# A gated DeltaNet kernel on one core: where the row coefficients of the triangular inverses are applied, and which engines make the right-hand sides

## The chip, the core and the metric

The kernel runs on one core of a Trainium2 chip. The core has a matrix engine (TensorE, in the profile PE, with its weight loads listed as PEld), a vector engine (VectorE, DVE), a scalar or activation engine (ScalarE, ACT), a general engine (GpSimd, POOL) and a queue engine that issues transfers (SyncE, SP). Each engine takes its instructions in order from its own queue and waits on semaphores for the others. The metric is the device time of one execution in microseconds (us), the median of several.

## What is computed

The reference is a two-layer diffusion backbone over 512 latent tokens and 256 context tokens of 1024 channels. Layer 0 mixes tokens with four bidirectional gated DeltaNet heads beside four pooling groups, layer 1 with convolutions; behind each mixer stands a ConvFFN. The change lies in the DeltaNet heads, and there in one term:

```python
def _gdn_chunk_terms(k, v, g, beta):          # per chunk of 64 tokens
    kb = k * beta
    a_mat = jnp.where(strict, jnp.einsum('bhnck,bhnsk->bhncs', kb, k) * decay, 0.0)
    rhs = jnp.concatenate([v * beta, kb * jnp.exp(gc)[..., None]], axis=-1)
    sol = lax.linalg.triangular_solve(a_mat + jnp.eye(GDN_CHUNK), rhs, left_side=True,
                                      lower=True, unit_diagonal=True)
```

Every chunk, head and direction needs the inverse of a unit triangular 64 x 64 matrix, whose off-diagonal part is the product of the keys with themselves, times a decay, times a coefficient beta for each row. The state recurrence then runs over the chunks, forward and backward.

## The kernel before, in words

**Matmuls.** The dense products are made in three passes. `piece` (L162) splits a block of weights: ScalarE writes the high part (L167), then GpSimd or VectorE the low part (L173). `gemm` (L210) issues the three products (L219).

**Order of the work.** Layer 0's mixer is a list of steps, `PLAN`: `b0 k0 k1 e0 q0 n0 e1 q1 v0 g0 i0 n1 v1 g1 x0 p0 p1 r1 ...`. The heads go in two pairs. `k` makes the keys, `e` (`systems`) their products with themselves times the decay, `m` (tile name `kk`), and the row coefficients `bl`, one table for each of three levels; `q` the queries. `e` ends with a small inverse of the 16 x 16 diagonal blocks (`base_inverse`), a serial chain on VectorE behind two transfers, whose result `gc` comes back from memory. `i0` runs the six inverse chains of head pair 0, three at a time; `x0` runs the two directions of pair 0's recurrence together with the six inverse chains of pair 1, four generators at a time; `r1` is pair 1's recurrence. In the trace these steps lie from about 150 to 330 us. Most instructions are put in order for each engine by the framework's scheduler, from the order of the code and the dependences; a few are pinned. Among the pinned ones are the products of `ada_rest` (L362) on VectorE, which reduce rows of a large weight for the modulation vectors: 24 are run inside `x0`, 16 inside `r1`, others in the output projection that follows (about 340 to 360 us).

**One inverse chain** (`inverse`, L974) doubles the inverted blocks three times, from 16 to 128 rows. Each level needs two matrix products. The first (`it_ps`, L991) multiplies `m` with a right-hand side `r1`, the second (`iv_ps`, L999) multiplies the masked result `it` (VectorE L993, at the last level ScalarE L995) with a right-hand side `r2`. The inverse `g` is then updated by VectorE (L1004) or, at the last level, ScalarE (L1002), and TensorE transposes it (L1006) to make the next level's `r1`. `r1` carries the row coefficients: it is the transposed inverse, times `bl` of the level, times a mask of zeros and ones. Since `bl` is a different scalar for each of the two heads, VectorE makes `r1` in two instructions of 128x128, one for each head: the first from `gc` (L984), those of the two later levels from PSUM (L1009). `r2` carries no coefficient, and GpSimd makes it in one instruction of 128x256 (L986 at first, L1011 later).

**Beside it.** `queries` squares the queries on ScalarE (`q_sq`, L1022), sums them on TensorE (`qn_ps`, L1025) and ends on VectorE (`qss`, L1036). The recurrence's ScalarE copies with a scale for each head, `kd` (L1069) and `vn` (L1089), each 128x128, run beside the chains of pair 1. Tiles of 128x256 come from rings: tag `inv` has ten buffers, three for each chain, tag `z` three.

Of the kernel before, what the change touches and what calls it, by code (L numbers as in the profile page):

```python
# [10 lines left out]
AF = mybir.ActivationFunctionType  # L11
# [3 lines left out]
P = 128  # L15
# [17 lines left out]
MUL, ADD, SUB = ALU.mult, ALU.add, ALU.subtract  # L33
# [81 lines left out]
class Kernel:  # L115
# [852 lines left out]
    def inverses(self, p, s):  # L968
        s["g"] = [self.t2("mg", "g") for _ in range(3)]
        two = lambda x, c: x[c // 2][:, 2 * (c % 2):2 * (c % 2) + 2]  # L970
        return [self.inverse(two(s["m"], c), s["gc"][:, :, 2 * c:2 * c + 2], s["bl"][:, :, 2 * c:2 * c + 2],
                             two(s["g"], c)) for c in (0, 1, 2, 5, 3, 4)]

    def inverse(self, m, gc, bl, g):  # L974


        nc = self.nc
        v4 = lambda x: x.rearrange("p q (b c) -> p q b c", c=16)
        mk = lambda m: m.rearrange("p (b c) -> p b c", c=16)
        mk4 = lambda m: mk(m)[:, None, :, :].broadcast_to([P, 2, 8, 16])  # L980
        gk = lambda k: gc[:, k][:, :, None, :].broadcast_to([P, 2, 8, 16])
        r1, r2, t = (self.t1("inv", nm) for nm in ("r1", "r2", "it"))
        for h in range(2):
            nc.vector.scalar_tensor_tensor(out=mk(r1[:, h]), in0=gc[:, 1, h][:, None, :].broadcast_to([P, 8, 16]),  # L984
                                           scalar=bl[:, 0, h:h + 1], in1=mk(self.par[:, 0]), op0=MUL, op1=MUL)
        nc.gpsimd.tensor_tensor(out=v4(r2), in0=gk(0), in1=mk4(self.par[:, 0]), op=MUL)  # L986
        nc.gpsimd.tensor_tensor(out=v4(g), in0=gk(0), in1=mk4(self.blk), op=MUL)
        for lv in range(3):
            pt = self.gd4("it_ps")
            for h in range(2):  # L990
                nc.tensor.matmul(out=pt[:, h], lhsT=m[:, h], rhs=r1[:, h], start=True, stop=True)  # L991
            if lv < 2:
                nc.vector.tensor_tensor(out=t, in0=pt[:, 0:2], in1=self.mask(self.lvl[:, lv], 2), op=MUL)  # L993
            else:
                nc.scalar.copy(out=t, in_=pt[:, 0:2])  # L995
            yield 1
            ps = self.gd4("iv_ps")
            for h in range(2):
                nc.tensor.matmul(out=ps[:, h], lhsT=t[:, h], rhs=r2[:, h], start=True, stop=True)  # L999
            if lv == 2:  # L1000
                for a, c in ((slice(0, 64), slice(64, P)), (slice(64, P), slice(0, 64))):
                    nc.scalar.activation(out=g[a, :, c], in_=ps[a, 0:2, c], func=AF.Copy, scale=-1.0)  # L1002
                break
            nc.vector.tensor_tensor(out=g, in0=g, in1=ps[:, 0:2], op=SUB)  # L1004
            for h in range(2):
                nc.tensor.transpose(out=ps[:, 2 + h], in_=g[:, h], identity=self.ident)  # L1006
            yield 1
            for h in range(2):
                nc.vector.scalar_tensor_tensor(out=r1[:, h], in0=ps[:, 2 + h], scalar=bl[:, lv + 1, h:h + 1],  # L1009
                                               in1=self.par[:, lv + 1], op0=MUL, op1=MUL)  # L1010
            (nc.gpsimd if R2 else nc.vector).tensor_tensor(out=r2, in0=g, in1=self.mask(self.par[:, lv + 1], 2), op=MUL)  # L1011

    def queries(self, p, s):
# [431 lines left out]
```

## Time and profile before

| | |
|---|---|
| time, median of 3 runs | 1320.72 us (1320.23 to 1323.22) |
| the profiled execution's own time | 1324.16 us |
| its span in the trace | 1322.4 us |
| mean granted TensorE clock | 0.981 |
| busy: TensorE, VectorE, GpSimd, ScalarE | 1262.9, 913.2, 669.1, 582.5 us |

A profile is one execution. Its page lists each engine's busy time, the span in 40 slices with the busy share in tenths (PEclk is the clock that TensorE was granted), the chain of work that ended last, and groups of instructions. A group's row reads: line, engine, operation, output tile and input tiles, shape, count, then busy time and the mean duration in ns, then the engine's idle time just before these instructions and what released it. A view of windows gives, for stretches of the span, each engine's busy time and count, the granted clock and the transfers' share.

### The profile page before, as it was taken

The page shows a single profiled execution, that of the slowest core. Times are in us where ns is not written, and L with a number is a line of the kernel's source. Part 1 is how long each engine was busy: PE and PEld are TensorE (multiplying, and loading weights), DVE is VectorE, ACT ScalarE, POOL GpSimd, SP SyncE. Part 2 cuts the span into 40 slices and gives each one's busy share as a digit, 9 for nine tenths or more (in the row PEclk, how much of TensorE's full clock was granted, in tenths as well). Part 3 has the DMA queues.
Part 4 walks back from the last instruction along what each step waited for, and adds up shares of the span by engine and source line. Part 5 has one row for each costly group of instructions (what it writes and reads, how often), then busy time and mean ns, then how long its engine had stood idle before and what let it go on. Part 6 is the DMA issues. An engine that isn't in the chain of part 4 may idle for free.

```text
span 1322.4 us, 19555 instructions
## 1 busy us (share of the span) xinstructions
PE 1262.9 (95%) x6690; PEld 1065.1 (81%) x6690; DVE 913.2 (69%) x1874; ACT 582.5 (44%) x1091; POOL 669.1 (51%) x607
## 2 busy tenths in 40 slices
PE   6998889989899999999999999899999999999996
PEld 2877878877798888888888988688988888888886
DVE  3778899998777878788444669847786666661135
ACT  3545324455547333333322685435653333332235
POOL 2355466666426555555354567954243434433452
PEclk8998899999999999999999999999999999999998
DMA  9511213431633656666565523234032233333334
GB/s 358 196 50 40 66 44 105 144 119 33 201 103 94 195 194 195 196 193 204 171 196 161 163 88 95 66 96 128 18 112 97 95 99 100 96 92 96 96 115 130
DMA packets 100340, 166.58 MB, mean 126 GB/s; under 512 B 20432, under 2 KB 25616, under 8 KB 100240
## 3 DMA queue, kind: packets, MB, share of 16 engines
q1 hardware_dynamic: 89280, 164.09, 38.5%
q10 hardware_dynamic: 10960, 1.25, 0.7%
q8 instruction: 53, 0.87, 0.3%
q14 instruction: 47, 0.39, 0.1%
HBM read 162.60 MB, written 2.69 MB: 125 GB/s over the span
## 4 chain that ended last, share of the span: by engine, by line
PE 65%; DVE 5%; ACT 2%; POOL 2%; issue 1%; DMA 1%; POOLq 0%; ACTq 0%; SPq 0%; DVEq 0%
PE prod_ps L219 40%; PE out_ps L219 20%; PE half_ps L219 3%; PE ln_e L417 1%; DVE z L478 1%; POOL w_lo L173 1%; PE ln_w L427 1%; DVE ln_d L424 1%; DMA ada_w<-in_ada 0%; DVE ada_w L362 0%; DVE ln_s L404 0%; DVE al L457 0%; ACT ln_u L490 0%; ACT w_hi L167 0%; DVE w_lo L173 0%
## 5 line engine op out<-in xcount | busy, mean ns | idle before, releaser
L173 POOL TENSOR_TENSOR w_lo<-w_raw,w_hi 128x512 fp32r<-128x512 f32 (+1 forms) x302 | 392.9, 1305 | 460.5 <-ACT w_hi L167 441.2
L167 ACT CAST w_hi<-w_raw 128x512 fp32r<-128x512 f32 (+1 forms) x408 | 246.3, 609 | 462.0 <-PE prod_ps L219 145.3
L219 PE MATMUL prod_ps<-uh,w_lo 128*128 128x512 f32 x792 | 309.9, 392 | 4.9 <-POOL w_lo L173 4.9
L219 PE MATMUL prod_ps<-uh,w_hi 128*128 128x512 f32 x792 | 309.7, 391 | 0.0
L219 PE MATMUL prod_ps<-ul,w_hi 128*128 128x512 f32 x792 | 309.4, 391 | 0.0
L604 DVE SCALAR_TENSOR_TENSOR f_acc<-prod_ps,prm,f_acc 128x441 f32<-128x441 f32 (+2 forms) x320 | 222.3, 695 | 61.5 <-ACT f_acc L593 52.2
L219 PEld LDWEIGHTS prod_ps<-uh,w_lo 128*128 128x128 f32 x792 | 149.4, 189 | 36.9 <-POOL w_lo L173 6.0
L219 PEld LDWEIGHTS prod_ps<-ul,w_hi 128*128 128x128 f32 x792 | 149.6, 189 | 31.2
L219 PEld LDWEIGHTS prod_ps<-uh,w_hi 128*128 128x128 f32 x792 | 149.6, 189 | 30.9
L173 DVE TENSOR_TENSOR w_lo<-w_raw,w_hi 128x512 fp32r<-128x512 f32 (+1 forms) x106 | 84.6, 798 | 124.4 <-ACT w_hi L167 120.9
L219 PE MATMUL out_ps<-ah,w_lo 128*128 128x256 f32 (+1 forms) x352 | 118.4, 336 | 4.6 <-DVE w_lo L173 4.6
L219 PE MATMUL out_ps<-ah,w_hi 128*128 128x256 f32 (+1 forms) x352 | 118.6, 337 | 1.6 <-ACT ah L456 1.6
L219 PE MATMUL out_ps<-al,w_hi 128*128 128x256 f32 (+1 forms) x352 | 119.4, 339 | 0.0
L219 PE MATMUL out_ps<-hh,w_lo 128*128 128x512 f32 (+1 forms) x280 | 99.3, 355 | 1.9 <-POOL w_lo L173 1.9
L219 PE MATMUL out_ps<-hh,w_hi 128*128 128x512 f32 (+1 forms) x280 | 98.7, 352 | 0.1
L219 PE MATMUL out_ps<-hl,w_hi 128*128 128x512 f32 (+1 forms) x280 | 98.6, 352 | 0.0
L362 DVE SCALAR_TENSOR_TENSOR ada_w<-ada_w,crow_ps 128x512 f32<-128x512 f32 x112 | 70.7, 682 | 9.8 <-DMA ada_w<-in_ada 9.8
L219 PEld LDWEIGHTS out_ps<-ah,w_lo 128*128 128x128 f32 x352 | 67.2, 191 | 11.9 <-DVE w_lo L173 4.8
L219 PEld LDWEIGHTS out_ps<-ah,w_hi 128*128 128x128 f32 x352 | 67.2, 191 | 8.7 <-ACT ah L456 2.0
L219 PEld LDWEIGHTS out_ps<-al,w_hi 128*128 128x128 f32 x352 | 67.5, 192 | 7.8 <-DVE al L457 0.8
L219 PEld LDWEIGHTS out_ps<-hh,w_lo 128*128 128x128 f32 x280 | 53.4, 191 | 9.9 <-POOL w_lo L173 2.2
L219 PEld LDWEIGHTS out_ps<-hh,w_hi 128*128 128x128 f32 x280 | 53.4, 191 | 7.9 <-ACT w_hi L167 0.3
(362 smaller groups left out, 2290.5 us busy)
## 6 DMA issues: line engine op xcount, KB each, us to landing
w_raw<-in_ffn_up SPq DMA_DIRECT2D x176, 256.0 KB, 2.6
ada_w<-in_ada SPq DMA_DIRECT2D x160, 256.0 KB, 3.7
w_raw<-in_ffn_down SPq DMA_DIRECT2D x100, 256.0 KB, 2.7
w_raw<-in_even_in SPq DMA_DIRECT2D x40, 256.0 KB, 2.7
w_raw<-in_odd_in SPq DMA_DIRECT2D x40, 256.0 KB, 2.8
ada_w<-in_ada SPq DMA_DIRECT2D x16, 512.0 KB, 8.4
w_raw<-in_even_out SPq DMA_DIRECT2D x16, 256.0 KB, 2.7
w_raw<-in_odd_out SPq DMA_DIRECT2D x16, 256.0 KB, 2.6
```

What stands on the lines that cost most here:

```text
L167: r = nc.scalar.copy(out=hi[:, :n], in_=raw)
L173: r = eng.tensor_tensor(out=lo[:, :n], in0=raw, in1=hi[:, :n].bitcast(F32), op=SUB)
L219: r = nc.tensor.matmul(out=o, lhsT=w, rhs=x[k][:, c0:c1], start=clear and k == i == 0, stop=k == n - 1 and i == 2, skip_group_check=pin)
L362: r = nc.vector.scalar_tensor_tensor(out=w, in0=w, scalar=1.0, in1=c, op0=MUL, op1=MUL, accum_out=self.mod[:, k, i:i + 1])
L417: nc.tensor.matmul(out=pe[:, 2 * (n * e + i):2 * (n * e + i) + 2], lhsT=t[:, i * P:(i + 1) * P], rhs=ones, start=e == 0 and i == 0 and not ...
L424: nc.vector.tensor_tensor(out=d[:, 0:n], in0=self.ident[:, None, :].broadcast_to([P, n, P]), in1=x.broadcast_to([P, n, P]), op=MUL)
L427: nc.tensor.matmul(out=o, lhsT=self.ones, rhs=d[:, 0:n].rearrange("p a b -> p (a b)"), start=True, stop=True)
L478: nc.vector.tensor_tensor(out=z, in0=z, in1=x, op=op)
L604: nc.vector.scalar_tensor_tensor(out=o, in0=sv[:, r0 + dr:r1 + dr, q0 + dc:q1 + dc], scalar=w[:, tap:tap + 1], in1=o, op0=MUL, op1=ADD)
```

## The change

The row coefficients move from `r1` to the other factor of the first product. A new function `rows` lets ScalarE write a copy of `m`, scaled with `bl` of the level, one 128x128 activation for each head, into a new tile `mb`; the product takes `mb` in place of `m`. `rows` is called ahead of the first level and, for each next level, before the chain's generator hands over. `r1` is then only a mask times the transposed inverse: the first one is one GpSimd instruction of 128x256, put ahead of the first `r2`; the later ones are one VectorE instruction of 128x256. `mb` is one tile a chain: from tag `z` for head pair 0, from tag `inv` for pair 1.

```diff
         return [self.inverse(two(s["m"], c), s["gc"][:, :, 2 * c:2 * c + 2], s["bl"][:, :, 2 * c:2 * c + 2],
-                             two(s["g"], c)) for c in (0, 1, 2, 5, 3, 4)]
+                             two(s["g"], c), "inv" if p else "z") for c in (0, 1, 2, 5, 3, 4)]
...
-    def inverse(self, m, gc, bl, g):
+    def inverse(self, m, gc, bl, g, tag):
...
-        for h in range(2):
-            nc.vector.scalar_tensor_tensor(out=mk(r1[:, h]), in0=gc[:, 1, h][:, None, :].broadcast_to([P, 8, 16]),
-                                           scalar=bl[:, 0, h:h + 1], in1=mk(self.par[:, 0]), op0=MUL, op1=MUL)
+        mb = self.t1(tag, "mb")
+        def rows(lv):
+            for h in range(2):
+                nc.scalar.activation(out=mb[:, h], in_=m[:, h], func=AF.Copy, scale=bl[:, lv, h:h + 1])
+        rows(0)
+        nc.gpsimd.tensor_tensor(out=v4(r1), in0=gk(1), in1=mk4(self.par[:, 0]), op=MUL)
...
-                nc.tensor.matmul(out=pt[:, h], lhsT=m[:, h], rhs=r1[:, h], start=True, stop=True)
+                nc.tensor.matmul(out=pt[:, h], lhsT=mb[:, h], rhs=r1[:, h], start=True, stop=True)
...
+            rows(lv + 1)
             yield 1
-            for h in range(2):
-                nc.vector.scalar_tensor_tensor(out=r1[:, h], in0=ps[:, 2 + h], scalar=bl[:, lv + 1, h:h + 1],
-                                               in1=self.par[:, lv + 1], op0=MUL, op1=MUL)
+            nc.vector.tensor_tensor(out=r1, in0=ps[:, 2:4], in1=self.mask(self.par[:, lv + 1], 2), op=MUL)
```

Lines behind the change stand five further down in the changed file: `q_sq` at L1022 before is L1027 after. The scheduler moves other instructions along with it. The first place is ScalarE's queue around the squares of the first pair of queries; `ql` are the queries, `vc` values, `w_hi` a split weight.

```order
 L805 ACTIVATE ql<-qkv_ps,prm 128x512
 L167 CAST w_hi<-w_raw 128x512 x2
-L1022 ACTIVATE q_sq<-ql 128x512 x2
+L988 ACTIVATE mb<-kk,bl 128x128 x4
+L1027 ACTIVATE q_sq<-ql 128x512 x2
 L805 ACTIVATE vc<-qkv_ps,prm 128x256
+L988 ACTIVATE mb<-kk,bl 128x128
 L811 ACT_TABLE_LOAD
 L811 ACTIVATE ql<-ql 128x512
```

Four scaled copies now stand ahead of the two squares, and a fifth behind the values.

The second place is GpSimd's queue at the start of `i0`, before the change; L986 is a first `r2`, L987 a first `g`, L1105 a mask of the recurrence.

```order
L932 MEMSET xi 128x512
L986 TENSOR_TENSOR r_1535<-gc,even_k 128x256
L933 MEMSET xi 128x2x16
L987 TENSOR_TENSOR g<-gc,even_k 128x256 x4
L173 TENSOR_TENSOR w_lo<-w_raw,w_hi 128x512 x5
L1105 TENSOR_TENSOR at<-el,even_k 128x256 x2
L986 TENSOR_TENSOR r_1546<-gc,even_k 128x256
L986 TENSOR_TENSOR r_1557<-gc,even_k 128x256
L1011 TENSOR_TENSOR r_1535<-g,even_k 128x256
```

The same place after the change, where L991 is the new first `r1` and L992 the first `r2`:

```order
L932 MEMSET xi 128x512
L991 TENSOR_TENSOR r_1534<-gc,even_k 128x256
L933 MEMSET xi 128x2x16
L992 TENSOR_TENSOR r_1535<-gc,even_k 128x256
L993 TENSOR_TENSOR g<-gc,even_k 128x256 x4
L173 TENSOR_TENSOR w_lo<-w_raw,w_hi 128x512 x4
L991 TENSOR_TENSOR r_1547<-gc,even_k 128x256
L992 TENSOR_TENSOR r_1548<-gc,even_k 128x256
L173 TENSOR_TENSOR w_lo<-w_raw,w_hi 128x512
L1110 TENSOR_TENSOR at<-el,even_k 128x256
L991 TENSOR_TENSOR r_1560<-gc,even_k 128x256
L992 TENSOR_TENSOR r_1561<-gc,even_k 128x256
```

Each chain's first `r1` stands right ahead of its `r2`; the second and third chain's come behind four and five weight splits.

The third place is VectorE's queue near the end of the output projection, before the change; `z` are the residual sums, `ln_s` the sums of the layer norm, and the last row is a split of weights that the next products need.

```order
L524 SCALAR_TENSOR_TENSOR z_3480<-out_ps,mod_g,z_3480 128x512
L362 SCALAR_TENSOR_TENSOR ada_w,mod<-ada_w,crow 128x512
L401 TENSOR_TENSOR ln_s_3621<-ln_s_3621,z_3480 128x512
L404 TENSOR_TENSOR ln_s_3622<-ln_s_3622,ln_sq 128x512
L524 SCALAR_TENSOR_TENSOR z_3481<-out_ps,mod_g,z_3481 128x512
L362 SCALAR_TENSOR_TENSOR ada_w,mod<-ada_w,crow 128x512
L401 TENSOR_TENSOR ln_s_3621<-ln_s_3621,z_3481 128x512
L404 TENSOR_TENSOR ln_s_3622<-ln_s_3622,ln_sq 128x512
L362 SCALAR_TENSOR_TENSOR ada_w,mod<-ada_w,crow 128x512 x2
L173 TENSOR_TENSOR w_lo<-w_raw,w_hi 128x512
```

The same place after the change:

```order
L524 SCALAR_TENSOR_TENSOR z_3528<-out_ps,mod_g,z_3528 128x512
L362 SCALAR_TENSOR_TENSOR ada_w,mod<-ada_w,crow 128x512
L401 TENSOR_TENSOR ln_s_3669<-ln_s_3669,z_3528 128x512
L404 TENSOR_TENSOR ln_s_3670<-ln_s_3670,ln_sq 128x512
L362 SCALAR_TENSOR_TENSOR ada_w,mod<-ada_w,crow 128x512
L524 SCALAR_TENSOR_TENSOR z_3529<-out_ps,mod_g,z_3529 128x512
L371 TENSOR_TENSOR mod_3749<-mod 128x16
L173 TENSOR_TENSOR w_lo<-w_raw,w_hi 128x512
L401 TENSOR_TENSOR ln_s_3669<-ln_s_3669,z_3529 128x512
L404 TENSOR_TENSOR ln_s_3670<-ln_s_3670,ln_sq 128x512
```

The split of the weights, which stood behind three rows of `ada_rest` and the `ln_s` sums of the last `z`, now stands two instructions behind that `z`, ahead of its sums; the rows of `ada_rest` stand further up.

## The prediction

> **What bounds the kernel now.** I read the page first: shares, slices and the chain that ended last.
>
> ```profile
> span 1322.4 us, 19555 instructions
> PE 1262.9 (95%) x6690; PEld 1065.1 (81%) x6690; DVE 913.2 (69%) x1874; ACT 582.5 (44%) x1091; POOL 669.1 (51%) x607
> ...
> PE   6998889989899999999999999899999999999996
> DVE  3778899998777878788444669847786666661135
> ...
> PE 65%; DVE 5%; ACT 2%; POOL 2%; issue 1%; DMA 1%; POOLq 0%; ACTq 0%; SPq 0%; DVEq 0%
> ```
>
> TensorE is busy 95% of the span and carries 65% of the chain that ended last. Over the whole kernel a lighter VectorE is worth nothing; it can pay only where TensorE has gaps. A slice is 33 us, so the inverse chains (150 to 330 us) are slices 5 to 10, where VectorE reads 8, 9, 9, 9, 9, 8. The view of windows gives these stretches, with two earlier and one later one that the new order touches.
>
> ```profile
> core 0: us, PE busy (x) PEld busy (x) DVE busy (x) ACT busy (x) POOL busy (x), PEclk, DMA share, GB/s
> 110.00:114.00 4.00, 1.12 (x10) 1.09 (x10) 3.32 (x6) 3.13 (x6) 2.11 (x2) 1.00 0.12 33
> 114.00:122.00 8.00, 8.00 (x34) 7.24 (x34) 7.41 (x23) 3.49 (x4) 1.76 (x3) 0.57 0.21 66
> 160.00:210.00 50.00, 46.11 (x305) 39.59 (x304) 47.13 (x108) 15.71 (x38) 28.87 (x37) 1.00 0.12 30
> 210.00:280.00 70.00, 65.72 (x457) 57.03 (x456) 65.25 (x182) 27.62 (x81) 48.30 (x57) 1.00 0.39 125
> 350.00:370.00 20.00, 15.36 (x108) 14.76 (x107) 17.29 (x34) 9.23 (x17) 7.84 (x6) 0.91 0.52 167
> ```
>
> Between 160 and 280 us, 120 us in all, VectorE is busy 47.13 + 65.25 = 112.38 and idle 7.62; TensorE is busy 111.83 and idle 8.17. Both are nearly full at once. The 8.17 us are what a faster supply can win here, as the trace counts it. ScalarE is busy 43.33 us of the 120 and GpSimd 77.17. The waits of this stretch tell which gaps are VectorE's; each row is total, times, longest.
>
> ```profile
> ACT w_hi L167 <- PE pool_ps L219: 17.0, 6, 5.8
> ACT it L995 <- PE it_ps L991: 15.0, 11, 7.7
> ...
> PE it_ps L991 <- DVE r L984: 3.6, 7, 1.0
> ...
> PE it_ps L991 <- DVE r L1009: 1.5, 3, 0.8
> ...
> PE k_ps L1064 <- DVE oo L1120: 0.8, 1, 0.8
> ...
> PE o_ps L1109 <- DVE s L1100: 0.7, 1, 0.7
> PE iv_ps L1006 <- DVE g L1004: 0.6, 2, 0.4
> ```
>
> Of the 8.17 us, 3.6 + 1.5 = 5.1 end with exactly the two groups that the change rewrites, and 2.1 with other VectorE work. So the ceiling in this stretch is small, whatever VectorE loses.
>
> **The change part by part.** The groups of the stretch from 160 to 280 us, kept apart by shape, price it.
>
> ```profile
> L362 DVE SCALAR_TENSOR_TENSOR ada_w<-ada_w,crow 128x512 f32<-128x512 f32 x26 | 22.9, 913 | 0.0
> L1011 POOL TENSOR_TENSOR r<-g,even_k 128x256 f32<-128x256 f32 x24 | 20.4, 864 | 11.9 <-DVE g L1004 11.8
> L1009 DVE SCALAR_TENSOR_TENSOR r<-iv_ps,bl,even_k 128x128 f32<-128x128 f32 x48 | 14.0, 340 | 0.5 <-PE iv_ps L1006 0.3
> L993 DVE TENSOR_TENSOR it<-it_ps,even_k 128x256 f32<-128x256 f32 x24 | 10.0, 420 | 2.9 <-PE it_ps L991 2.6
> ```
>
> From 145 to 330 us, which holds all of the first right-hand sides and of the recurrence's scaled copies:
>
> ```profile
> L984 DVE SCALAR_TENSOR_TENSOR r<-gc,bl,even_k 128x128 f32<-128x128 f32 x24 | 13.8, 603 | 4.1 <-DMA gc<-scr 4.1
> ...
> L1089 ACT ACTIVATE vn<-v_ps,nb 128x128 f32<-128x128 f32 x40 | 11.9, 366 | 9.3 <-PE v_ps L1086 9.2
> ...
> L1069 ACT ACTIVATE kd<-k_ps,gc_ex 128x128 f32<-128x128 f32 x40 | 11.0, 385 | 2.3 <-PE k_ps L1064 2.3
> ...
> L986 POOL TENSOR_TENSOR r<-gc,even_k 128x256 f32<-128x256 f32 x12 | 9.4, 792 | 5.2 <-DMA gc<-scr 5.2
> ```
>
> And the lines of the two right-hand sides by themselves, with the shortest, median and longest in ns:
>
> ```profile
> L984 DVE SCALAR_TENSOR_TENSOR r<-gc,bl,even_k x24: 335/490/1392, 149.4 to 261.5; 128x128 f32<-128x128 f32 x24
> L1009 DVE SCALAR_TENSOR_TENSOR r<-iv_ps,bl,even_k x48: 330/340/352, 180.5 to 273.2; 128x128 f32<-128x128 f32 x48
> ```
>
> *The first right-hand side leaves VectorE.* VectorE loses 24 instructions, 13.8 us by the group's busy time. GpSimd gains 12, at the price of its twin L986, 0.79 us each: 9.5 us. In GpSimd's order the new one stands ahead of that twin, and `it_ps` and `iv_ps`, in the rows above, wait for VectorE and never for GpSimd. I therefore let the 3.6 us that TensorE waits for L984 go. What is late next is the first `it_ps` behind GpSimd, where the second and third chain's instruction stands behind four or five splits of weights; a rival prices that. GpSimd's 43 us of idle time in the stretch cover the 9.5 us.
>
> *The later ones become one instruction.* Instead of two of 0.34 us there is one of 128x256 with a PSUM and an SBUF input; L993 has exactly these operands, 0.42 us. VectorE saves 14.0 − 24 × 0.42 = 4.0 us in all. On the chain from `g` to the next `it_ps` the last half is ready 0.26 us sooner, and TensorE waited there three times, 1.5 us: at 0.17 us each (0.26 less something for the first half, which could start early before) I take 0.5.
>
> *What VectorE's 18 us are worth.* VectorE loses 13.8 + 4.0 = 17.8 us, more than twice what TensorE idles here. Beyond the two waits above, the freed time can shorten only the 2.1 us of the other waits on VectorE. I take half, 1.0; the bounds are nothing and 2.1.
>
> *ScalarE's copies.* There are 72 new activations (12 chains, three levels, two heads). The trace has no scaled copy from SBUF to SBUF of this size; the nearest rows are `vn` and `kd`, 128x128 with a scale from PSUM. Each group's busy time over its count, 11.9 / 40 and 11.0 / 40, gives 0.30 and 0.28 us where they follow each other, and the mean is 0.37 alone. So 72 cost 20 to 27 us of ScalarE, which idles 77 us of the 120. I cost them at nothing where they come a level ahead: `mb` needs only `m` and `bl`, known long before. The cover fails where ScalarE's queue stands behind something that waits for TensorE; that is the first rival.
>
> *Four copies ahead of the squares.* This is one place where the copies are on a path. The order has four `mb` ahead of `q_sq`, at 112 us of the trace.
>
> ```profile
> 111.20 1.13 ACT L167 CAST w_hi<-w_raw 128x512 fp32r<-128x512 f32 x2
> ...
> 112.23 1.15 ACT L1022 ACTIVATE q_sq<-ql 128x512 f32<-128x512 f32 x2
> ...
> 112.91 1.05 PE L1025 MATMUL qn_ps<-ones,q_sq 128*128 128x2 f32 x8 [2.88 <-ACT q_sq L1022]
> ...
> 115.95 0.17 DVE L1036 TENSOR_SCALAR qss<-qn_ps 128x8 f32<-128x8 f32 x1
> ```
>
> ScalarE goes straight from the casts to the squares, and TensorE waits 2.88 us for them. Four copies of 0.30 us put the squares 1.2 us later, with nothing to hide it on TensorE, which has nothing else in this window (1.12 us busy of 4). VectorE's `qss` stands in the middle of the serial base inverse, so the delay also moves that chain. I take +1.2; the bounds are 0, if the scheduler's other moves give it back, and 1.5 (4 × 0.37).
>
> The row for 114 to 122 us shows a granted clock of 0.57 right behind that gap. The clock is lowered there already, and I let a longer gap cost itself and no second fall.
>
> *The end of the output projection.* The split of weights that TensorE waits for there moves ahead of two `ln_s` sums and of rows of `ada_rest`.
>
> ```profile
> 351.86 0.68 DVE L401 TENSOR_TENSOR ln_s<-ln_s,z 128x512 f32<-128x512 f32 x1
> 352.46 0.68 DVE L404 TENSOR_TENSOR ln_s<-ln_s,ln_sq 128x512 f32<-128x512 f32 x1
> ...
> 356.41 0.68 DVE L173 TENSOR_TENSOR w_lo<-w_raw,w_hi 128x512 fp32r<-128x512 f32 x1
> ```
>
> and TensorE's side of it:
>
> ```profile
> 357.15 0.46 PE L219 MATMUL out_ps<-ah,w_lo 128*128 128x256 f32 x1 [4.64 <-DVE w_lo L173]
> ```
>
> The rows of `ada_rest` still have to run ahead of it, only earlier; the two sums, 1.36 us, do not. TensorE's 4.64 us can shrink by that, if the rows' transfers don't hold VectorE instead. I take −1.0, between 0 and −1.4.
>
> *Sum.* −3.6 − 0.5 − 1.0 + 1.2 − 1.0 = −4.9 us. Against the profiled execution (1324.16 us, of which 1.8 lie around the span) that is 1319.3. That execution lies 3.4 us above the median of the runs, 1320.72, and I take the sum off the median: 1315.8.
>
> [...] L984, with two operands in SBUF, runs from 335 to 1392 ns, while L1009, with one, keeps within 330 to 352; and L362, two operands from SBUF, has a mean of 913 ns in this stretch. So VectorE's work with two SBUF operands is stretched by something. [...]
>
> **The rivals.**
>
> *Slower: the products wait for ScalarE.* `mb` sits in an in-order queue behind work that itself waits for TensorE: casts that wait for the pooling products (17.0 us in 6 waits, 2.8 each, longest 5.8) and `it` copies of the last level (15.0 us in 11 waits, longest 7.7). Where an `mb` of the next level stands behind one, its chain's `it_ps` comes late by up to that wait, and only three or four chains run beside each other to cover it. Two such exposed waits of 2.9 us undo the 4.9; four give −4.9 + 11.6 = +6.7, about 1327. For it: the copies are made in the same turn as the transposes, just when the level needs them next. Against it: with a level of other chains between, most waits will have passed. 0.18.
>
> *No measurable change: TensorE's order or GpSimd is the bound.* The waits for L984 go, but the first `r1` of the later chains, behind splits of weights on GpSimd, is late in its place, or the gap comes up at the next in-order matmul. The 5.1 us then only change their name, and the sum keeps +1.2 − 1.0: about 1320.5. For it: VectorE and TensorE idle about the same, 7.62 and 8.17. Against it: the first `r1` does not depend on anything that is late. 0.26.
>
> *Faster by more.* Matmuls overlap in the records, so that a busy TensorE may hide slack. Were VectorE the real bound of the stretch, more than half of its 17.8 us would come off: with the other terms about −10, 1310.7. For it: VectorE is 94% busy from 160 to 280 us. Against it: every wait for VectorE there comes to only 7.2 us. 0.14.
>
> **How the numbers follow.** My forecast, −4.9 us with its own range of −3 to −7, has 0.42; the rivals 0.18, 0.26 and 0.14. A measurement of this kernel can tell about 0.2%, 2.6 us. The forecast and the larger gain are faster by more than that: 0.56; no measurable change 0.26; slower 0.18. The range reaches to the larger gain, 1310.0, and on the slow side past no change into the first rival's smaller cases, three exposed waits, −4.9 + 8.7 = +3.8: 1324.0. That leaves out the rest of both tails.
>
> **What would show it.** The waits of TensorE on the first right-hand sides should be gone and no wait of `it_ps` on GpSimd or ScalarE should take their place; a total above 2.9 us there means a rival. `mb` should show 72 activations of 0.28 to 0.37 us, the single product 24 of 0.42 us, the new GpSimd row 12 of about 0.79. VectorE's busy time should fall by about 18 us; if it falls by under 12, the rows of L362 have been stretched. The gap ahead of `qn_ps` should read about 4.1 us instead of 2.88, and the wait of `out_ps` at the end of the projection about 3.6 instead of 4.64. I am wrong if TensorE's waits between 160 and 330 us stay at their sum, or if the place where the time moves lies outside the inverse chains.

## The result, and the profile after

The changed kernel takes 1329.49 us (median of 6, 1324.64 to 1333.74) against 1320.61 (median of 6, 1319.87 to 1323.22): a ratio of 1.0057, 95% interval 1.0038 to 1.0075. It is slower, by 8.9 us of the medians. A second measurement (e1 below) gave 1329.91 against 1321.91, 1.0067 (1.0045 to 1.0088).

The two profiled executions hide this. That of before took 1324.16 us, longer than any of its six runs; that of after took 1324.64, the shortest of its runs. So places are read from the traces, and sizes from the medians. The page of after:

```profile
span 1322.8 us, 19607 instructions
...
PE 1260.1 (95%) x6690; PEld 1063.7 (80%) x6690; DVE 895.3 (68%) x1826; ACT 604.1 (46%) x1163; POOL 680.9 (51%) x619
...
PE   6998899987989999999999999899999999999997
...
DVE  3778897996777887778444669847686666661125
```

VectorE did lose what was forecast, 913.2 − 895.3 = 17.9 us (forecast 17.8), ScalarE gained 21.6 and GpSimd 11.8. TensorE's row is what differs: in its tenth slice, 298 to 331 us, it has a 7 where before had a 9, and the inverse chains are over by then. The windows of after, of the stretch of the chains and of that place:

```profile
core 0: us, PE busy (x) PEld busy (x) DVE busy (x) ACT busy (x) POOL busy (x), PEclk, DMA share, GB/s
160.00:210.00 50.00, 47.31 (x317) 40.97 (x316) 40.57 (x85) 28.03 (x80) 34.70 (x44) 1.00 0.16 43
210.00:280.00 70.00, 63.77 (x457) 56.14 (x455) 65.50 (x171) 37.34 (x115) 53.62 (x60) 1.00 0.41 127
325.00:330.00 5.00, 0.91 (x1) 0.50 (x2) 4.00 (x5) 0.00 (x0) 3.94 (x3) 0.54 0.15 53
330.00:335.00 5.00, 5.00 (x24) 3.53 (x23) 3.37 (x13) 2.17 (x4) 0.00 (x0) 0.78 0.17 52
```

From 160 to 280 us TensorE idles 120 − 111.08 = 8.92 us, where it idled 8.17 before: the lighter VectorE closed no gap of TensorE. Between 325 and 330 us TensorE is busy 0.91 of 5 us, and behind it the granted clock is at 0.54 and 0.78. The waits of after between 145 and 345 us name both:

```profile
ACT mb L988 <- PE it_ps L997: 18.9, 11, 3.7
...
PE pool_y L1192 <- DVE pool_o L1186: 6.7, 1, 6.7
...
DVE pool_o L1181 <- POOL pool_q L1177: 5.7, 1, 5.7
...
PE it_ps L997 <- POOL r L991: 2.0, 1, 2.0
...
PE it_ps L997 <- DVE r L1015: 1.8, 4, 0.6
```

The 5.1 us in which `it_ps` waited for VectorE's right-hand sides have become 2.0 for GpSimd's first one and 1.8 for the new single product. And one wait of 6.7 us is new: `pool_y`, the last product of the fourth pooling, a stage that the diff doesn't touch. How it comes about is in three lines of each trace: the chains' first products, the recurrence's last ones and the poolings' products, with the first and last start. Before:

```profile
L991 PE MATMUL it_ps<-r,kk x144: 270/275/378, 163.5 to 274.3; 128*128 128x128 f32 x144
L1112 PE MATMUL o_ps<-vn,at x64: 274/275/276, 242.6 to 319.1; 128*128 128x128 f32 x64
L219 PE MATMUL pool_ps<-ah,w_lo x32: 387/398/482, 208.7 to 309.3; 128*128 128x512 f32 x32
```

After:

```profile
L997 PE MATMUL it_ps<-r,mb x144: 270/275/377, 162.8 to 268.2; 128*128 128x128 f32 x144
L1117 PE MATMUL o_ps<-vn,at x64: 275/275/275, 238.5 to 312.4; 128*128 128x128 f32 x64
L219 PE MATMUL pool_ps<-ah,w_lo x32: 388/397/482, 206.9 to 315.7; 128*128 128x512 f32 x32
```

The chains end 6.1 us earlier and the recurrence 6.7 us earlier. That is not time won. The windows from 150 us to the recurrence's end, before and after:

```profile
150.00:319.50 169.50, 156.82 (x1050) 137.07 (x1051) 158.45 (x415) 68.51 (x186) 110.57 (x126) 0.97 0.29 89
150.00:312.80 162.80, 149.49 (x1026) 131.64 (x1027) 142.75 (x366) 86.29 (x249) 111.08 (x131) 0.98 0.29 89
```

TensorE idles 12.7 us there before and 13.3 after; what has shrunk is its work, by 24 matmuls, 22 of them dense products (of L219 246 before, 224 after). TensorE works in the order that was fixed when the kernel was built (the traces of after and e1, two executions of the same kernel, show the same one from 150 to 350 us), and the products of poolings and gates are what fills it between the recurrence's steps. In the order of the changed kernel fewer of them stand ahead of the recurrence's end and more behind it: the fourth pooling's last product starts 9.8 us ahead of the recurrence's last one before, and 3.3 us behind it after. Its result has a serial tail on the other engines, in after's timeline:

```profile
317.24 0.58 ACT L1173 COPY pool_b<-pool_ps 128x512 f32<-128x512 f32 x1
...
318.84 1.24 POOL L1177 TENSOR_TENSOR pool_q<-pool_b 128x527 f32<-128x527 f32 x1
320.16 2.20 POOL L1177 TENSOR_TENSOR pool_q<-pool_q 128x525 f32<-128x525 f32 x2
...
323.54 1.28 POOL L1177 TENSOR_TENSOR pool_q<-pool_q 128x513 f32<-128x513 f32 x1
...
324.86 1.73 DVE L1181 SCALAR_TENSOR_TENSOR pool_o<-pool_q,pool_b 128x512 f32<-128x512 f32 x1 [5.70 <-POOL pool_q L1177]
...
329.09 1.22 PE L1192 MATMUL pool_y<-pool_o,even_k 128*128 128x512 f32 x1 [6.66 <-DVE pool_o L1186]
```

From the end of the product (316 us) to `pool_y` (329) lie 13 us, and TensorE's order has one gate, 24 products of 0.23 us, to put there. Before, that tail ran under the recurrence.

### The profile page after: what moved, and what is told of

Its sections match the earlier page's. It is cut to its first block, busy times and chain, and to the rows that moved or that the text cites. A ratio compares the mean times of both kernels' runs of the same rounds, so it can differ in the third digit from the quotient of the medians.

```text
span 1322.8 us, 19607 instructions
## 1 busy us (share of the span) xinstructions
PE 1260.1 (95%) x6690; PEld 1063.7 (80%) x6690; DVE 895.3 (68%) x1826; ACT 604.1 (46%) x1163; POOL 680.9 (51%) x619
## 4 chain that ended last, share of the span: by engine, by line
PE 66%; DVE 4%; POOL 3%; ACT 2%; issue 1%; DMA 1%; ACTq 0%; SPq 0%; POOLq 0%; DVEq 0%
PE prod_ps L219 40%; PE out_ps L219 20%; PE half_ps L219 3%; PE ln_e L417 1%; POOL w_lo L173 1%; DVE z L478 1%; PE ln_w L427 1%; DVE ada_w L362 0%; ACT w_hi L167 0%; DVE ln_s L404 0%; DVE w_lo L173 0%; POOL al L457 0%; POOL pool_q L1177 0%; POOL conf_far L1230 0%; DMA ada_w<-in_ada 0%
## 5 line engine op out<-in xcount | busy, mean ns | idle before, releaser
L219 PE MATMUL prod_ps<-uh,w_lo 128*128 128x512 f32 x792 | 309.7, 391 | 4.9 <-POOL w_lo L173 4.9
L219 PE MATMUL prod_ps<-uh,w_hi 128*128 128x512 f32 x792 | 309.4, 391 | 0.0
L219 PE MATMUL prod_ps<-ul,w_hi 128*128 128x512 f32 x792 | 309.3, 391 | 0.0
L219 PEld LDWEIGHTS prod_ps<-uh,w_lo 128*128 128x128 f32 x792 | 149.2, 188 | 37.0 <-POOL w_lo L173 5.9
L219 PEld LDWEIGHTS prod_ps<-ul,w_hi 128*128 128x128 f32 x792 | 149.5, 189 | 31.2
L219 PEld LDWEIGHTS prod_ps<-uh,w_hi 128*128 128x128 f32 x792 | 149.5, 189 | 31.1
L219 PE MATMUL out_ps<-ah,w_lo 128*128 128x256 f32 (+1 forms) x352 | 118.4, 336 | 0.6 <-DVE w_lo L173 0.6
L219 PE MATMUL out_ps<-al,w_hi 128*128 128x256 f32 (+1 forms) x352 | 118.9, 338 | 0.0
L219 PE MATMUL out_ps<-ah,w_hi 128*128 128x256 f32 (+1 forms) x352 | 118.3, 337 | 0.0
L219 PE MATMUL out_ps<-hh,w_lo 128*128 128x512 f32 (+1 forms) x280 | 98.5, 352 | 1.9 <-POOL w_lo L173 1.9
L219 PE MATMUL out_ps<-hh,w_hi 128*128 128x512 f32 (+1 forms) x280 | 98.0, 350 | 0.1
L219 PE MATMUL out_ps<-hl,w_hi 128*128 128x512 f32 (+1 forms) x280 | 97.8, 349 | 0.0
L219 PEld LDWEIGHTS out_ps<-ah,w_lo 128*128 128x128 f32 x352 | 67.0, 190 | 8.0 <-DVE w_lo L173 0.8
L219 PEld LDWEIGHTS out_ps<-al,w_hi 128*128 128x128 f32 x352 | 67.3, 191 | 7.5 <-issue 0.5
L219 PEld LDWEIGHTS out_ps<-ah,w_hi 128*128 128x128 f32 x352 | 66.9, 190 | 7.0 <-issue 0.2
L219 PEld LDWEIGHTS out_ps<-hh,w_lo 128*128 128x128 f32 x280 | 52.6, 188 | 9.7 <-POOL w_lo L173 2.1
L219 PEld LDWEIGHTS out_ps<-hh,w_hi 128*128 128x128 f32 x280 | 52.7, 188 | 7.9 <-ACT w_hi L167 0.3
```

What stands on the lines that cost most here:

```text
L219: r = nc.tensor.matmul(out=o, lhsT=w, rhs=x[k][:, c0:c1], start=clear and k == i == 0, stop=k == n - 1 and i == 2, skip_group_check=pin)
```

## The experiments

Each was run beside the kernel before on the same chip; its medians in the five measurements were 1321.91 (e1 to e4), 1322.80 (e5 to e8), 1320.77 (e9 to e12), 1322.14 (e13 to e16) and 1321.81 (e17). Theory 1: the change makes the inverse chains shorter, but the order that follows from it leaves a hole at the end of the mixer. Theory 2: the loss is at the four copies ahead of the squares.

**e1, the changed kernel again.**

> The changed kernel as it is, a second time, for its spread and a second trace. Theory 1 (the stretch from 150 to 320 us is some 6.7 us shorter, and TensorE then stands 6.66 us before the last pooling product, after which its clock drops): the same hole before pool_y, and over the single executions the span falls as the mean clock rises, about 1 us for each 0.001, from 0.983 at 1323 us to 0.974 at 1332 us. Theory 2 (the four scaled copies ahead of the squares are the cost): the gap before the first qn_ps is about 4.0 us in both traces, and the long executions have their lowered clock behind it, between 113 and 160 us. Median 1327 to 1331 either way.

1329.91 us, six executions from 1327.01 to 1333.68. The hole is there again, and the gap before the squares' sums. Two gaps of e1:

```profile
113.98 1.86 PE L1030 MATMUL qn_ps<-ones,q_sq 128*128 128x2 f32 x8 [4.00 <-ACT q_sq L1027]
...
332.12 2.08 PE L1192 MATMUL pool_y<-pool_o,even_k 128*128 128x512 f32 x2 [6.66 <-DVE pool_o L1186]
```

Over its executions the span falls with the mean clock, from 0.975 to 0.979, by 1.4 us for each 0.001; in the first measurement, from 0.974 to 0.983, by 1.0. The median clock of e1 is 0.976, that of before beside it 0.983. At 1.0 to 1.4 us each, these 0.007 are 7 to 10 us, so the loss goes along with a lower clock; which gap brings it, the next runs tell.

**e2, the fourth pooling early.** One step of the list is moved.

```diff
-PLAN = '... x0 p0 p1 r1 p2 g2 w2 p3 w0 g3 w3 d0 w1 d1 a20'
+PLAN = '... x0 p0 p1 r1 p2 p3 g2 w2 w0 g3 w3 d0 w1 d1 a20'
```

> The changed kernel with one step moved in the list: the fourth pooling (p3) is put directly behind the third, ahead of the gates g2 and g3, so that both gates' 48 products stand behind it in TensorE's order. Theory 1: the 6.66 us hole before pool_y goes to under 1 us and the lowered clock behind it as well; time 1316 to 1320, faster than the kernel before by the 3 to 5 us that the inverse chains gained. Theory 2: the hole goes, but the time stays above the kernel before, 1322 to 1327, since the squares and the clock behind them are as they were.

1323.69 us, ratio 1.0014 (0.9996 to 1.0032): 6.2 us less than e1, and no longer measurably slower than before. No wait of 0.9 us or more stands before `pool_y`, and the stretch behind is full:

```profile
325.00:330.00 5.00, 4.79 (x25) 3.14 (x23) 4.57 (x15) 4.95 (x7) 2.50 (x2) 1.00 0.29 102
330.00:335.00 5.00, 4.20 (x18) 3.19 (x19) 4.73 (x9) 3.98 (x10) 3.00 (x2) 1.00 0.41 133
```

The size of the repair is as theory 1 has it; the end is not, since 1316 to 1320 was expected, and 1323.69 lies in theory 2's range, whose cause e3 tests. The hole was most of the loss, and a gain was not behind it. The wait of `out_ps` for `w_lo` is 3.5 us in this trace.

**e3, the squares first.** The squares and the first level's copies of pair 0 are pinned in the order of the code.

```diff
...
+                if tag == "z" and lv == 0:
+                    self.tc.keep_in_program_order(r)
...
+            if p == 0:
+                self.tc.keep_in_program_order(r)
```

> The changed kernel with the squares of the queries pinned ahead of the first level's scaled copies on ScalarE; the order at the end of the mixer stays, with the pooling product late. Theory 1: the gap before the first qn_ps falls from 3.98 to about 2.9 us, and the time falls by 1 to 2 us only, to about 1327 to 1329. Theory 2: the time falls back to that of the kernel before or lower, 1317 to 1321, although the hole before pool_y stays near 6.7 us.

1330.21 us, 1.0059 (1.0036 to 1.0083). The gap before `qn_ps` fell to 3.06 us, the hole stayed at 6.65, the time stayed at e1's. Theory 2 falls as the cause of the loss; the 1 to 2 us that theory 1 expected here are not seen either.

**e4, control: before with the pooling early** (the list of e2).

> Control: the kernel before, with the same step moved in the list. Theory 1: no hole stood there before, so the move is worth nothing or little, 1318 to 1322. If the move by itself is worth 5 us or more here, then what it wins in the changed kernel is not a hole that the change opened. Theory 2 expects the same 1318 to 1322.

1323.14 us, 1.0013 (1.0000 to 1.0026). Where the change has not been made, the move gains nothing: the median is 1.2 us longer, the interval goes from nothing to 3.4. Where it has been made, the move is worth 6.2 us. So the hole is the change's own.

**e5, useless work in the hole.**

```diff
...
+        if h == 3:
+            self.gemm(self.mm("fill_ps"), ws, self.ah, self.al, 0, T)
```

> The changed kernel with useless work in the hole: 24 more products of 128x512 (the last gate's, a second time, into a bank that nobody reads) stand between the last gate and the last pooling product, about 24 x 0.227 = 5.4 us of TensorE. Theory 1, clock part (the hole costs twice, once by its length and once by the two windows of half clock behind it, 3.4 us): the hole shrinks to about 1.2 us, pool_y comes at the same time as without the work, the 3.4 us of lost clock between 320 and 345 us go, and the kernel gets faster by about 3, to 1326 or 1327, although it does more. Rival (the clock has nothing to do with the hole): the time stays at 1329 to 1331.

1330.47 us, 1.0059 (1.0042 to 1.0076). The 5.4 us of extra work cost nothing, and in the trace the clock stays up where it fell:

```profile
325.00:330.00 5.00, 5.00 (x26) 3.89 (x25) 2.96 (x7) 2.38 (x4) 4.71 (x4) 1.00 0.04 4
330.00:335.00 5.00, 4.87 (x26) 3.32 (x23) 5.00 (x17) 4.18 (x8) 2.25 (x3) 1.00 0.56 176
```

But the 3 us that I expected to win back did not come; the time is the rival's. The output projection began at 331.3 us instead of 333.7 and gave that back before its layer norm, whose first product waited 4.23 us (3.52 in after). That the clock behind the hole costs on its own is not shown by the time.

**e6, the first right-hand side on VectorE** (one line; alone).

```diff
-        nc.gpsimd.tensor_tensor(out=v4(r1), in0=gk(1), in1=mk4(self.par[:, 0]), op=MUL)
+        nc.vector.tensor_tensor(out=v4(r1), in0=gk(1), in1=mk4(self.par[:, 0]), op=MUL)
```

> One part of the change undone: the first right-hand side goes back from GpSimd to VectorE, as one product of 128x256 without the coefficient; the rest as changed, the late pooling product too. Theory 1 with GpSimd as its second place (the third chain's first product stands 2.0 us behind GpSimd's queue, and one window of half clock, 1.7 us, follows it): that wait goes, the clock between 165 and 200 us stays at 1.00, time 1325 to 1328, the hole before pool_y as it was. Rival (GpSimd's queue is no part of the loss; the wait only changes its name): 1329 to 1331.

1333.92 us, 1.0083 (1.0067 to 1.0100): 4 us more than e1 by the medians, with intervals that overlap (e1 1.0045 to 1.0088), and more than either side expected. The wait for GpSimd goes and others come in its place; of TensorE's waits of e6 between 160 and 300 us:

```profile
PE it_ps L997 <- DVE r L1015: 2.5, 4, 0.9
PE k_ps L1069 <- DVE oo L1125: 2.4, 1, 2.4
PE it_ps L997 <- DVE r L991: 2.2, 3, 1.1
```

But the two traces don't put the loss there. The first product of the output projection's layer norm starts at 372.7 us in e6 and at 372.2 in after, while e6's span is 9.6 us longer (1332.4 against 1322.8). Behind that product e6's granted clock is lowered more often, in stages that the edit doesn't touch:

```profile
372.70:384.00 11.30, 11.30 (x55) 11.12 (x55) 4.37 (x15) 2.90 (x5) 0.00 (x0) 0.55 0.06 21
933.00:940.00 7.00, 7.00 (x34) 6.82 (x33) 2.07 (x8) 1.15 (x2) 0.00 (x0) 0.51 0.00 0
```

In after the clock reads 0.86 from 372.2 to 384 us and 1.00 in the second window. A trace is one execution; where the 4 us of the medians come from is open.

**e7, both repairs** (e2 and e6).

> Both repairs: the fourth pooling early in the list, and the first right-hand side on VectorE. Theory 1 with GpSimd's queue as second place: 1323.7 less 2.0 of wait and 1.7 of clock, 1319 to 1321. Rival (what is left of the loss is the gap before the squares): 1323 to 1325.

1328.76 us, 1.0036 (1.0023 to 1.0049), 5 us above e2, and again the intervals overlap. It points the same way as e6.

**e8, all three repairs** (e2, e3 and e6).

> All three repairs: the fourth pooling early, the first right-hand side on VectorE, the squares of the queries ahead of the scaled copies. If the inverse chains gain anything on TensorE's side, it must show here, since every new gap is gone: theory 1 then gives 1316 to 1319. If TensorE's own work bounds the stretch and VectorE's lost 18 us are worth nothing, the time is that of the kernel before, 1320 to 1323.

1323.87 us, 1.0014 (0.9996 to 1.0031). Nothing gained over before. It also takes back what e6 and e7 seemed to say. Beside e12 below, which differs from it only in the engine of the first right-hand side (1323.03), it is not measurably slower, although its trace has e6's waits again (`it_ps` 2.1 and 1.8 us, `k_ps` 2.4). And against e7 the pinned squares are worth 4.9 us, where they are worth nothing in e3 and e12. Each edit also makes the framework order other instructions anew, so a difference of 4 to 5 us between two of these kernels is not the price of one part.

**e9, a lighter VectorE without the change.** 22 products of `ada_rest` are left out of the control e4, so that part of the modulation is not computed; GpSimd clears the table that they would have filled.

```diff
...
+        nc.gpsimd.memset(self.mod, 0.0)
...
-                        self.ada_rest(1, True)
+                        if i == 0 and self.ada_next:
+                            self.ada_next += 1
+                        else:
+                            self.ada_rest(1, True)
```

> The control of the kernel before (fourth pooling early), with 22 of the 24 products of ada_rest that run on VectorE beside the second set of inverse chains left out, so that part of the modulation is not computed: VectorE loses 22 x 0.91 = 20 us in that stretch, more than the change takes off it, and nothing else is touched. If VectorE's load bounds the stretch (what the prediction's larger gain and half of its 1.0 us rested on): 1313 or lower against the control's 1323. If TensorE's own work bounds it (theory 1): 1320 to 1324, within 3 us of the control, and VectorE's idle time in the trace grows instead.

1329.20 us, 1.0057 (1.0038 to 1.0076): 6 us slower than its control with 20 us less to do, which neither side had expected. Here too the chains end sooner and the time is longer, with nothing of the change in the kernel; but the place is another. The chains' first products and the recurrence's last ones:

```profile
L995 PE MATMUL it_ps<-r,kk x144: 270/275/377, 162.8 to 261.1; 128*128 128x128 f32 x144
L1116 PE MATMUL o_ps<-vn,at x64: 275/275/421, 234.0 to 321.3; 128*128 128x128 f32 x64
```

and the waits between 270 and 315 us:

```profile
PE v_ps L1090 <- DVE n L1084: 7.6, 2, 4.4
DVE pool_o L1180 <- POOL pool_q L1176: 6.8, 2, 4.4
...
PE k_ps L1080 <- DVE s L1101: 3.6, 1, 3.6
```

The chains end 12 us sooner than in the control (261.1 against 273.2), and the recurrence ends where it did (321.3 against 321.8), because the pooling steps now stand among its steps in VectorE's queue: VectorE waits 6.8 us for GpSimd's `pool_q` with the recurrence's `n` and `s` behind it. So neither branch of the expectation is shown.

**e10, ScalarE's copies doubled** (in e2's kernel).

```diff
-                nc.scalar.activation(out=mb[:, h], in_=m[:, h], func=AF.Copy, scale=bl[:, lv, h:h + 1])
+                for _ in range(2):
+                    nc.scalar.activation(out=mb[:, h], in_=m[:, h], func=AF.Copy, scale=bl[:, lv, h:h + 1])
```

> The changed kernel with the fourth pooling early, and each of ScalarE's 72 scaled copies made twice: 24 us more on ScalarE. If ScalarE's queue is a cost of the change (the prediction's slower rival), the time grows by 3 to 10 us over the 1323.7 of the same kernel with single copies, with waits of it_ps on mb. Theory 1 (the copies are covered except the first four, ahead of the squares): 1324 to 1326, the gap before the first qn_ps 1.2 us longer.

1327.33 us, 1.0040 (1.0023 to 1.0056), 3.6 above e2 by the medians, with intervals that overlap. ScalarE's busy time is 624.5 us in the trace, where e2's has 604.2. Only four copies stand ahead of the squares, as in after, so the gap there did not grow (3.77 us); `it_ps` waited for `mb` 0.7 us in all. The time is in the rival's range without the rival's waits, and some gate products stand in other places of TensorE's order than in e2. So 20 us more of ScalarE may not be quite free. How much the single copies cost is open.

**e11, the last pooling product behind the transposes.**

```diff
-PLAN = '... p2 g2 w2 p3 w0 g3 w3 d0 w1 d1 a20'
+PLAN = '... p2 g2 w2 p3 w0 g3 d0 w1 d1 w3 a20'
```

> The changed kernel with another repair of the hole: the last pooling's product (w3) is put behind both heads' output transposes (d1), so that TensorE has the transposes to do while the pooling is made; the pooling itself stays where the change put it. Theory 1: the 6.66 us hole shrinks by what the 8 transposes and their waits take, to 3 to 5 us, and the time to 1325 to 1328. If the hole is not the cost: 1329 to 1331.

1331.77 us, 1.0072 (1.0053 to 1.0090): no gain. The waits between 318 and 340 us say why:

```profile
DVE pool_o L1181 <- POOL pool_q L1177: 5.7, 1, 5.7
PE ot_ps L1151 <- DVE gate L1156: 5.4, 1, 5.4
```

The hole has only changed its name. VectorE stands at `pool_o` in its own order, and what it has to do for the transposes (`gate`) stands behind that. The late pooling is the cause on two engines, not the one product.

**e12, pooling early and squares first** (e2 and e3).

> Two repairs with the first right-hand side left on GpSimd, as the change has it: the fourth pooling early, and the squares pinned ahead of the scaled copies. Against the 1323.7 of the first repair alone: if the 1.1 us of longer gap before the squares, and a window of half clock with it, cost what the prediction said, 1320 to 1322.5. If the gap before the squares is worth nothing measurable: 1322.5 to 1325.

1323.03 us, 1.0009 (0.9991 to 1.0026). Here, as in e3, the squares are worth nothing measurable.

**e13 to e17, giving the freed time something to do.** With the pooling early the change brings nothing (e2, e8, e12), although VectorE has 18 us less to do. In e13 three more calls of `ada_rest`, six products, move out of the output projection into the stretch (the last step of the list, `a20`, which brings the calls up to 20, becomes `a23`); in e14 VectorE also takes three of ten weight splits of the mixer from GpSimd. e15 and e17 are the same edits on the kernel before (with e4's list); e16 has the splits alone.

```diff
-AX0 = 12
+AX0 = 15
...
-SHARE_EVEN = 0.1
+SHARE_EVEN = 0.3
```

> The changed kernel with the fourth pooling early and the squares first (1323.0 in the run before this), and three more calls of ada_rest, six products on VectorE, inside the stretch of the chains instead of in the output projection. If the freed time of VectorE is worth what is put into it: the wait of TensorE for w_lo near the end of the output projection (3.3 us, with a window of half clock) goes, the stretch keeps its length, time 1317 to 1320. If VectorE's time there is worth nothing because the order of each engine, not its load, sets the stretch: 1321 to 1326, with the gain at the end lost again in the stretch.

> As e13, and VectorE takes three of ten weight splits in the mixer instead of one of ten, so that GpSimd's queue ahead of the later chains' first right-hand sides is two splits shorter. If the freed time is worth what is put into it: the 2.0 us wait of it_ps on GpSimd goes too, with its window of half clock, 1314 to 1318. If not: 1321 to 1327.

> Control of e13: the kernel before with the fourth pooling early (1323.1), and the same six products of ada_rest moved into the stretch, where VectorE is 94% busy. If VectorE's load there matters: the stretch grows by about 6 x 0.9 = 5 us, what the output projection gains is undone, 1321 to 1327. If its load does not matter: it gains as e13 does, 1317 to 1320.

> The changed kernel with the fourth pooling early and the squares first, and three of ten weight splits in the mixer on VectorE instead of one; ada_rest as it was. If the wait of it_ps on GpSimd's queue was a cost of its own: 1319 to 1321.5. If it only changes its name, as with the first right-hand side on VectorE: 1322 to 1327.

> Control of e14: the kernel before with the same edits (fourth pooling early, six products of ada_rest inside the stretch, three of ten weight splits on VectorE). If VectorE's freed 18 us are what e14 spends: VectorE is overfull here, the chains end later than in e15 (it_ps last at 279.7 us), 1324 to 1330. If the edits are good by themselves: 1314 to 1319.

| | with the change | without it |
|---|---|---|
| pooling early | e2 1323.69, 1.0014 (0.9996 to 1.0032) | e4 1323.14, 1.0013 (1.0000 to 1.0026) |
| and ada_rest moved | e13 1319.21, 0.9984 (0.9965 to 1.0002) | e15 1324.58, 1.0021 (1.0011 to 1.0030) |
| and splits moved too | e14 1316.24, 0.9959 (0.9941 to 0.9976) | e17 1330.25, 1.0052 (1.0037 to 1.0068) |

(e13, e14 and e16 also have the squares first.) e16 alone gave 1323.80, 1.0018 (1.0004 to 1.0032). The two columns go apart, by 14 us of the medians at the end, and in the last two rows their intervals don't overlap. e14 beats the kernel before by 5.9 us, and the same edits without the change cost 8.4, each beside before on its own chip. The chains' first products, in e14 and then in e17:

```profile
L999 PE MATMUL it_ps<-r,mb x144: 270/275/377, 164.2 to 273.3; 128*128 128x128 f32 x144
```

```profile
L991 PE MATMUL it_ps<-r,kk x144: 270/275/377, 167.4 to 285.5; 128*128 128x128 f32 x144
```

With the change the chains end at 273.3 us, where before had them (274.3), and the output projection is rid of its longest wait: in e14 TensorE's waits between 330 and 370 us are

```profile
PE ln_e L417 <- DVE ln_s L401: 1.0, 1, 1.0
...
PE out_ps L219 <- ACT ah L456: 0.8, 1, 0.8
```

in place of the 4.64 us for `w_lo`. That wait is gone in e17 as well, so the columns part in the stretch: without the change the chains end 11 us later than in the kernel before, at 285.5. e13 came out as its first branch says (though its interval just reaches no gain over before), e15 and e16 as their slower ones, e14 and e17 as the freed time has it: with more work put on VectorE its load does lengthen the stretch, and the change makes room for that work.

## Why the prediction was wrong, by its steps

*The waits for the first right-hand sides, −3.6 us.* This step failed first. The waits for L984 went, but GpSimd's instruction for the third chain stood behind weight splits and `it_ps` waited 2.0 us for it, once. That was the second rival's place, at less than its price; TensorE's idle time from 160 to 280 us rose from 8.17 to 8.92 us. Whether VectorE would have been the better place, e6 to e8 and e12 leave open.

*The single product, −0.5.* Its size was right, 24 of 0.416 us, but `it_ps` waits for it 1.8 us where it waited 1.5.

*VectorE's 18 us, worth 1.0.* VectorE lost 17.9 us, as forecast, and that closed no gap of TensorE. Inside the stretch the rows of `ada_rest` grew; three rows of after, from 160 to 280 us:

```profile
L362 DVE SCALAR_TENSOR_TENSOR ada_w<-ada_w,crow 128x512 f32<-128x512 f32 x30 | 33.0, 1131 | 0.0
L988 ACT ACTIVATE mb<-kk,bl 128x128 f32<-128x128 f32 x66 | 22.1, 401 | 18.9 <-PE it_ps L997 18.9
...
L1015 DVE TENSOR_TENSOR r<-iv_ps,even_k 128x256 f32<-128x256 f32 x24 | 9.5, 416 | 0.9 <-PE iv_ps L1012 0.8
```

The mean of `ada_rest` in the stretch is 1131 ns instead of 913, 6.5 us over these 30. How much of it comes from the twelve new GpSimd instructions is not shown: e1, the same kernel as after, has 1069 ns in the stretch, and e6, where they are back on VectorE, still 1037.

*What the freed time does* is where the forecast failed in kind. I priced it by TensorE's waits inside the stretch and looked for what gets late in its place there. The new order instead has less of the filling work inside the stretch, and what stands behind it had a long tail with nothing beside it: 6.7 us of hole, 6.2 us of the time by e2. None of my rivals named it. Both signs that I gave for being wrong came: TensorE idles no less in the stretch, and the time moves at a place outside the inverse chains. I had quoted three places of the order; the fourth, TensorE's order at the end of the recurrence, has the fourth pooling ahead of 18 gate products before the change and 15 of its own 24 products behind the recurrence after it. It could be read before the run.

*The slower rival* forecast 1327 and had 0.18, and the result is on its side for another reason: `it_ps` waits for `mb` 0.3 us in all of after's trace, although `mb` itself waits 18.9 us in 11 places. Its mechanism did not occur, and that its number is near is luck. A copy takes a mean of 0.40 us, somewhat above my 0.28 to 0.37. e10 leaves the copies a small part at most.

*The copies ahead of the squares, +1.2.* The gap is as forecast, 3.98 to 4.05 us where I said 4.1. Its cost is not seen in the time: e3 changed nothing, and e12 was 0.7 us below e2, within the intervals. Only beside e7 did e8 come out faster, with the order of other instructions changed too.

*The end of the output projection, −1.0.* The wait for `w_lo` fell by more than forecast, from 4.64 to 0.6 us in after, and a wait of the layer norm (3.52 us instead of 0.78) took its place, which I had not asked for.

*No measurable change* would have been the right forecast for the change with its hole closed: 1323.0 to 1323.9 in e2, e8 and e12 against 1323.1 in e4. What stays open is why the framework's order puts less of the filling work ahead of the recurrence's end, what the engine of the first right-hand side is worth, and what the single copies cost.

## What to carry to other kernels

Time taken off an engine that is not the bound is worth what is put into its place: here 18 us of VectorE were first worth less than nothing, then, with the hole closed, nothing, and once they were filled 5.9 us against the kernel before and 14 against the same edits without the change. Where a fixed order mixes a serial part with filling work, an earlier end of the serial part can be filling work moved behind it: count the bound engine's work and idle time up to that end before calling it a gain. Read in the order of the bound engine what now stands last, and whether its tail has anything to run beside. A transfer of the same edit to the kernel before (e4, e15, e17) is the run that tells a repair from an improvement.

## What the runs showed of the hardware

The same program takes 1324.64 to 1333.74 us, and the mean granted clock goes with it, from 0.983 to 0.974. In after, the wait for GpSimd's first right-hand side (2.03 us, to 172.14 us) left the clock at 1.00 (so it reads from 158.2 to 325.3 us); in e1 the same wait, 2.10 us, did not:

```profile
175.10 1.10 PE L997 MATMUL it_ps<-r,mb 128*128 128x128 f32 x4 [2.10 <-POOL r L991]
```

The windows of e1 there, and around the hole:

```profile
171.86:175.27 3.41, 1.30 (x12) 1.11 (x11) 1.92 (x5) 0.56 (x1) 3.36 (x4) 1.00 0.20 75
175.27:178.69 3.42, 3.42 (x17) 3.42 (x18) 2.36 (x6) 0.80 (x2) 2.85 (x4) 0.50 0.01 2
...
325.00:330.00 5.00, 0.46 (x3) 0.03 (x1) 2.08 (x2) 2.50 (x3) 5.00 (x5) 0.89 0.00 0
330.00:335.00 5.00, 2.88 (x7) 1.75 (x8) 2.40 (x6) 0.69 (x1) 1.96 (x2) 0.50 0.35 105
335.00:340.00 5.00, 5.00 (x26) 3.83 (x25) 4.83 (x18) 3.24 (x7) 0.93 (x1) 0.93 0.11 35
```

The missing clock is 3.42 × 0.50 = 1.7 us behind the short wait and 5 × (0.11 + 0.50 + 0.07) = 3.4 us at the hole, and 5 × (0.46 + 0.22) = 3.4 us at the hole of after as well. In these three places it comes in pieces of 1.7 us: the clock is at 0.50 for 3.42 us behind e1's short wait, and from 325.4 to 332.2 us, 6.8 us, at the hole of after. But the same wait of about 2 us cost a piece in one execution and none in another.

In e2 and e5 the wait is 2.11 and 2.10 us long and ends at 173.17 and 171.79 us. The clock of e2 reads 0.87 from 170 to 175 us and 0.79 from 175 to 180, that of e5 0.73 and 0.93: 5 × (0.13 + 0.21) and 5 × (0.27 + 0.07), one piece of 1.7 us each time. What sets after apart from e1, e2 and e5 is not shown; no run moves the wait alone.
